# Two unsplit blocks ahead of the units in a feed-forward network, and GpSimd additions in its norm (Trainium2)

## The chip, the cores and the metric

The kernel runs on one core of one Trainium2 chip. The metric is the device time of one execution in microseconds (us); lower is better. Three runs of the kernel before gave 1261.36, 1261.36 and 1261.72 us, median 1261.36 us.

## The reference

Two layers of a decoder run on 16 learned meta tokens followed by 512 tokens (528 columns), width 1024. Each layer normalises `h`, projects it once for a forgetting-attention group (8 heads) and a retention group (4 heads), joins both groups through an output projection that is added to `h`, and adds a gated feed-forward network of width 2816. All arithmetic is float32.

```python
xn = rmsnorm(h, attn_norm_g)
proj = xn @ w_in                          # q, k, v of both groups, gates
mix = concat(fox_attention(...), silu(rg) * head_groupnorm(retention(...)))
h = h + mix @ w_out
hn = rmsnorm(h, ffn_norm_g)
ff = silu(hn @ w_gate) * (hn @ w_up)      # 1024 -> 2816
h = h + ff @ w_down                       # after layer 2: rmsnorm, meta tokens dropped
```

## The kernel before, in words

**Layout.** `h` lies transposed: eight tiles `h0` to `h7` of 128 features by 528 columns. Every float32 operand is split into a rounded part (type fp32r, names ending in `hi` or `h`) and the rest (`lo`, `l`), and each product is three TensorE matmuls: hi by hi, hi by lo, lo by hi. In layer 0 a pass over the 528 columns is two matmuls of 264 columns; in layer 1, where the meta tokens are no longer needed, it is one of 512.

**Weights.** A weight block of 128x1024 arrives by DMA in a tile `raw`. ScalarE casts it into `whi` (L199), and VectorE, or GpSimd where `dense_steps` was called with `pool`, subtracts to give `wlo` (L202; GpSimd in pieces of 128 columns). `convert` does this for the next block while a block is multiplied (L225); `ahead=(1, 4)` says at which of its steps.

**Feed-forward network.** The 2816 features are 22 blocks of 128. The first `PLAIN` blocks are plain: the gate product and the up product, eight steps of k each. Each later block is a `Unit`, in which gate and up share work in the manner of Strassen and Winograd: seven products of four chunks with three matmuls each over half of the columns (264 or 256), 84 matmuls in all. `head` uses `x` as it is; `middle` and part of `tail` need the four token forms `th`, `tl`, which `x_forms` (L883 and following) makes from `h` on ScalarE and VectorE; the weight sums of a unit (`make2` to `make4`, L961 and following) are VectorE's too. Blocks are grouped in `ROUNDS`; while one round is computed, the blocks of the round before are multiplied by `w_down` (`down`, L1065), a pair of output tiles for each unit. At the end of layer 1 the last round is `down` in two column parts of 272 and 240 (L930), with the final norm beside it.

**The norm of the feed-forward network.** `squares` takes the eight squares of `h` on ScalarE (L352, L357) and sums them by seven additions into `ss` on VectorE (L361). `sqh` and `sql`, the split of that sum, go through a matmul with ones (L304) that TensorE meets after the twelfth step of the network. `scale_split` makes `xh` (ScalarE, L339) and `xl` (VectorE, L341), the split input; step k of the first block needs `xh` and `xl` of tile k. `add_h` (L832, L829) has just added the output projection to `h`. `squares` is called with `att=False` in three places: for the feed-forward norm of layer 0 and of layer 1, and for the attention norm of layer 0 at the very start of the program, where it is also pinned in program order. The attention norm of layer 1 passes `att=True`.

**What sets the order.** TensorE runs its instructions in the order in which the steps are written; the other engines' orders come from the scheduler, by priority, and each engine executes its own queue strictly in order. Pools of tiles with a fixed number of buffers make a writer wait for the readers of the buffer's last content: three for `raw`, two for `whi` and `wlo`, four for the group of temporaries that holds `sq`. In PSUM, `psum()` (L267) hands out two buffers of a pair of banks, `psd`, and `psum_a()` (L270) four single banks, `psa`. A unit's two sums that `middle` and `tail` share accumulate in one `psd` pair, from its head to its `done`, where VectorE reads it (L1006, `sg`). The second `down` of a fill takes a `psd` pair as well; the first takes two `psa` banks in layer 0, by its last argument, and a `psd` pair in layer 1.

## Time and profile before

| | |
|---|---|
| median of three runs | 1261.36 us |
| the profiled execution | 1261.38 us, its span 1259.6 us |
| TensorE busy | 1248.7 us, 9225 matmuls |
| VectorE busy | 989.2 us |
| ScalarE busy | 706.6 us |
| GpSimd busy | 281.6 us |

In the profile PE is TensorE, PEld its weight loads, DVE VectorE, ACT ScalarE, POOL GpSimd and SP the engine that issues most DMAs. Times are us from the start of the span, which is 1.8 us shorter than the time of the execution. Matmuls overlap: a row's duration is longer than the distance to the next one, and the distance is what a matmul costs. A row of the timeline gives the start, the length, the engine and line, what is written and read, and how many instructions it merges; idle time in front stands in brackets with what ended it. Layer 0's feed-forward network starts at 281.6 us, layer 1's at 903.3 us.

### The profile page before, as it was taken

How to read it: one execution, taken by the hardware profiler on the slowest of the kernel's cores; microseconds unless marked ns; L12 is line 12 of the kernel's file. 1: busy time of each engine (PE TensorE's matmuls, PEld its weight loads, DVE VectorE, ACT ScalarE, POOL GpSimd, SP SyncE). 2: the span in 40 equal slices, each digit the busy share in tenths (PEclk: the TensorE clock that was granted, in tenths of full speed). 3: DMA queues.
4: the chain of work that ended last, by engine and by line, in shares of the span. 5: the costliest groups of instructions: out<-in, count | busy, mean ns of one | idle time of the engine just before them, and what ended most of it. 6: DMA issues, size and time to landing. Idle time of an engine off the chain costs nothing.

```text
span 1259.6 us, 23534 instructions
## 1 busy us (share of the span) xinstructions
PE 1248.7 (99%) x9225; PEld 1191.9 (95%) x9225; DVE 989.2 (79%) x1786; ACT 706.6 (56%) x1307; POOL 281.6 (22%) x552
## 2 busy tenths in 40 slices
PE   9999999999999999999999999999999999999997
PEld 8999999999999999999999988998789999999996
DVE  7887756789888888887786876567899888888867
ACT  7767655776454444444466665557764444444445
POOL 4545655420000000000125556554100000000000
PEclk9999999999999999999999999999999999999999
DMA  6222222123233323332322222221333333333322
GB/s 219 68 76 71 74 68 90 55 81 117 93 102 103 96 100 101 101 101 85 103 75 84 76 77 70 82 77 51 130 95 111 101 101 101 100 101 101 101 84 67
DMA packets 43342, 116.19 MB, mean 92 GB/s; under 512 B 5088, under 2 KB 12000, under 8 KB 43232
## 3 DMA queue, kind: packets, MB, share of 16 engines
q1 hardware_dynamic: 42800, 114.41, 28.4%
q8 instruction: 72, 1.18, 0.4%
q14 instruction: 38, 0.31, 0.1%
q10 hardware_dynamic: 432, 0.29, 0.1%
HBM read 112.58 MB, written 2.10 MB: 91 GB/s over the span
## 4 chain that ended last, share of the span: by engine, by line
PE 95%; DVE 3%; ACT 2%; DMA 0%; issue 0%; ACTq 0%; DVEq 0%
PE psd L225 31%; PE psa L930 18%; PE psd L1065 14%; PE psd L930 13%; PE psa L225 5%; PE psa L1065 4%; PE psa L441 2%; PE psa L608 2%; PE psa L538 1%; PE psa L742 1%; PE psa L778 1%; PE psa L402 1%; PE psa L304 0%; DMA raw<-w_in 0%; PE psa L617 0%
## 5 line engine op out<-in xcount | busy, mean ns | idle before, releaser
L202 POOL TENSOR_TENSOR wlo<-raw,whi 128x128 fp32r<-128x128 f32 x504 | 262.4, 555 | 243.0 <-ACT whi L199 220.9
L225 PE MATMUL psd<-xh,whi 128*128 128x264 f32 (+1 forms) x792 | 195.2, 314 | 0.1
L225 PE MATMUL psd<-xh,wlo 128*128 128x264 f32 (+1 forms) x792 | 186.6, 303 | 0.0
L225 PE MATMUL psd<-xl,whi 128*128 128x264 f32 (+1 forms) x792 | 186.2, 302 | 0.2 <-DVE xl L341 0.2
L225 PEld LDWEIGHTS psd<-xh,wlo 128*128 128x128 f32 x792 | 126.8, 188 | 6.3 <-DVE wlo L202 0.4
L225 PEld LDWEIGHTS psd<-xh,whi 128*128 128x128 f32 x792 | 128.1, 189 | 4.9 <-ACT whi L199 0.6
L225 PEld LDWEIGHTS psd<-xl,whi 128*128 128x128 f32 x792 | 127.3, 188 | 4.8 <-DVE xl L341 0.9
L199 ACT CAST whi<-raw 128x512 fp32r<-128x512 f32 (+1 forms) x168 | 98.2, 613 | 42.9 <-PE psd L225 29.2
L918 ACT CAST whi<-raw 128x1024 fp32r<-128x1024 f32 (+2 forms) x62 | 54.9, 885 | 51.3 <-PE psd L930 39.8
L918 ACT CAST fwhi<-raw 128x1024 fp32r<-128x1024 f32 (+2 forms) x62 | 55.6, 897 | 47.5 <-PE psd L930 40.0
L122 POOL MEMSET kc<- 64x528 f32 x4 | 2.1, 533 | 345.6 <-PE psa L930 345.4
L919 DVE TENSOR_TENSOR wlo<-raw,whi 128x1024 fp32r<-128x1024 f32 (+2 forms) x62 | 62.9, 1015 | 12.3 <-ACT whi L918 12.2
L919 DVE TENSOR_TENSOR fwlo<-raw,fwhi 128x1024 fp32r<-128x1024 f32 (+2 forms) x62 | 64.0, 1032 | 10.1 <-ACT fwhi L918 10.0
L930 PE MATMUL psa<-th,whi 128*128 128x264 f32 (+1 forms) x232 | 65.4, 282 | 0.0
L930 PE MATMUL psa<-th,wlo 128*128 128x264 f32 (+1 forms) x232 | 65.4, 282 | 0.0
L930 PE MATMUL psa<-tl,whi 128*128 128x264 f32 (+1 forms) x232 | 65.3, 282 | 0.0
L930 PE MATMUL psa<-th,fwhi 128*128 128x264 f32 (+1 forms) x224 | 63.4, 283 | 0.0
L930 PE MATMUL psa<-tl,fwhi 128*128 128x264 f32 (+1 forms) x224 | 63.3, 283 | 0.0
L930 PE MATMUL psa<-th,fwlo 128*128 128x264 f32 (+1 forms) x224 | 63.2, 282 | 0.0
L555 ACT ACTIVATE pr<-pr,nmax 128x144 f32<-128x144 f32 (+1 forms) x64 | 36.8, 576 | 45.5 <-DVE nmax L542 26.0
L918 ACT CAST fwhi<-S 128x1024 fp32r<-128x1024 f32 x20 | 21.0, 1049 | 68.6 <-PE psa L930 66.5
L996 ACT COPY e<-psa 128x264 f32<-128x264 f32 (+1 forms) x114 | 42.8, 375 | 28.3 <-PE psa L930 24.1
(366 smaller groups left out, 4041.1 us busy)
## 6 DMA issues: line engine op xcount, KB each, us to landing
raw<-w_in SPq DMA_DIRECT2D x54, 512.0 KB, 3.5
raw<-w_gate SPq DMA_DIRECT2D x44, 512.0 KB, 3.9
fraw<-w_up SPq DMA_DIRECT2D x38, 512.0 KB, 3.5
raw<-w_down SPq DMA_DIRECT2D x64, 256.0 KB, 2.9
raw<-w_out SPq DMA_DIRECT2D x16, 512.0 KB, 3.5
raw<-w_down SPq DMA_DIRECT2D x32, 192.0 KB, 2.5
raw<-w_up SPq DMA_DIRECT2D x6, 512.0 KB, 3.5
h<-x_t SPq DMA_DIRECT2D x8, 264.0 KB, 4.9
```

Source lines behind the costliest of these rows:

```text
L199: pin(nc.scalar.copy(hi, job["raw"][:, c0:c1]), pinned)
L202: pin(sub(lo[:, c:c + step], job["raw"][:, c0 + c:c0 + c + step], hi[:, c:c + step].bitcast(F32)), pinned)
L225: nc.tensor.matmul(ps[1][b][:, 0:c1 - c0], w[:, wk, :], x[:, c0:c1], start=(k == 0 and i == 0), stop=(k == n - 1 and i == 2))
L402: nc.tensor.matmul(ps[:, 0:c1 - c0], wf[k // HB][:, k % HB, :], st["x"][k][part][:, c0:c1], start=(i == 0), stop=(i == 2 * NK - 1))
L441: nc.tensor.transpose(ps[:, 128 * j:128 * j + 128], src[:, o:o + 128], idt)
L555: nc.scalar.activation(pr, pr, AF.Exp, bias=nmax[0:nq], scale=-1.0, accum_out=rsum)
L608: nc.tensor.matmul(po[:, c0:SEQ], v[:, j, :], pp[:, j, META + c0:T], start=(j == 0 and i == 0), stop=(j == 4))
L918: nc.scalar.copy(hi, src)
L919: nc.vector.tensor_sub(lo, src, hi.bitcast(F32))
L930: nc.tensor.matmul(bank()[:, 0:b.shape[-1]], a[:, o + k, :], b, start=(fresh and k == 0 and i == 0), stop=(k == n - 1 and i == 2), skip_gr ...
L996: nc.scalar.copy(self.t["e"][:, i], self.t["x"][:, 0:w])
L1065: nc.tensor.matmul(v[:, 0:c1 - c0], a[:, s * n + k, :], b[:, c0:c1], start=(k == 0 and i == 0), stop=(k == n - 1 and i == 2))
```

## The change

- `PLAIN` goes from 3 to 2, so block 2 becomes a unit in both layers, and the rounds become one of two blocks and five of four (before: 3, 4, 4, 4, 4, 3).
- The heads of the first two units are both issued before the first `middle`; the code that carried a unit's tail over to the next one goes, since there are always `down` fills.
- `x_forms` are inserted every seven steps, not nine.
- In `squares`, where `att` is false, the additions of squares 1 to 5 go to GpSimd; 6 and 7 stay on VectorE.
- `whi` and `wlo` get three buffers; blocks marked `far` convert the weights two blocks ahead; the third `w_out` block of the second round is subtracted on GpSimd. The second sums of the first unit are made at high priority.
- Of the `down` fills, the first for each of the first two units of layer 1 uses two banks and halves of 256 columns.

```diff
-ROUNDS = ((0, 3), (3, 7), (7, 11), (11, 15), (15, 19), (19, 22))
-PLAIN = 3
+ROUNDS = ((0, 2), (2, 6), (6, 10), (10, 14), (14, 18), (18, 22))
+PLAIN = 2
...
-        return pool.tile([128, NK, 128], F32R, name=tag, tag=tag, bufs=2)
+        return pool.tile([128, NK, 128], F32R, name=tag, tag=tag, bufs=2 if tag[0] == "f" else 3)
...
-                [(NK, *[wp.tile([128, NK, 128], F32R, name=i, tag=i) for i in ("whi", "wlo")])]
+                [(NK, *[wring(i) for i in ("whi", "wlo")])]
...
                         convert(j + 1, 4 * half + 4)
+                        if far:
+                            convert(j + 2, 4 * half + 4)
...
                 with ExitStack() if att else tc.high_priority():
-                    nc.vector.tensor_add(acc[:, c], acc[:, c], sq[:, c])
+                    (nc.vector if att or k > 5 else nc.gpsimd).tensor_add(acc[:, c], acc[:, c], sq[:, c])
...
-                                rnd == 0 or m2 < 2, rnd == 1 and m2 == 1) for m2 in range(NK // 2)], [])
+                                rnd == 0 or m2 < 3, rnd == 1 and m2 == 1, far=rnd == 1 and m2 > 1) for m2 in range(NK // 2)], [])
...
-                nc.vector.tensor_add(s[:, HB:NK], b[:, 0:HB], b[:, HB:NK])
-                nc.vector.tensor_sub(s[:, 0:HB], s[:, HB:NK], a[:, 0:HB])
-                splits(hi, lo, s)
+                with tc.high_priority() if self.f == PLAIN else ExitStack():
+                    nc.vector.tensor_add(s[:, HB:NK], b[:, 0:HB], b[:, HB:NK])
+                    nc.vector.tensor_sub(s[:, 0:HB], s[:, HB:NK], a[:, 0:HB])
+                    splits(hi, lo, s)
...
-                u = Unit(f)
-                steps += u.head()
-                for v in tails:
-                    v.last()
-                    steps += v.tail()
-                tails = []
+                for i in (f, f + 1) if f == PLAIN else (f,):
+                    if i not in units:
+                        units[i] = Unit(i)
+                        steps += units[i].head()
+                u = units[f]
                 u.rest()
                 steps += u.middle()
...
+                steps += down(j, 0, 2 * p, g0, g1, not real or f < PLAIN + 2)
...
-            steps.insert(NK + 4 + 9 * i, x_forms(i))
+            steps.insert(NK + 4 + 7 * i, x_forms(i))
```

The first place is VectorE at the start of the program, the sum of the squares for layer 0's attention norm (`ss` is the sum, `sq` a square, `mxl` the low part of the third weight block, `sql` the low part of the sum). Before:

```order
L361 TENSOR_TENSOR ss_217<-ss_217,sq_219 128x528
L361 TENSOR_TENSOR ss_217<-ss_217,sq_222 128x528
L361 TENSOR_TENSOR ss_217<-ss_217,sq_225 128x528
L361 TENSOR_TENSOR ss_217<-ss_217,sq_228 128x528
L396 TENSOR_TENSOR pick_83<-idt_81 40x8
L361 TENSOR_TENSOR ss_217<-ss_217,sq_231 128x528
L361 TENSOR_TENSOR ss_217<-ss_217,sq_234 128x528
L202 TENSOR_TENSOR mxl0_329<-raw_326,mxh0_328 128x512
L361 TENSOR_TENSOR ss_217<-ss_217,sq_237 128x528
L202 TENSOR_TENSOR mxl1_331<-raw_326,mxh1_330 128x512
L295 TENSOR_TENSOR sql_337<-ss_217,sqh_336 128x528
```

The same place on VectorE with the change:

```order
L398 TENSOR_TENSOR pick_83<-idt_81 40x8
L363 TENSOR_TENSOR ss_217<-ss_217,sq_234 128x528
L363 TENSOR_TENSOR ss_217<-ss_217,sq_237 128x528
L202 TENSOR_TENSOR mxl0_329<-raw_326,mxh0_328 128x512
L202 TENSOR_TENSOR mxl1_331<-raw_326,mxh1_330 128x512
L297 TENSOR_TENSOR sql_337<-ss_217,sqh_336 128x528
```

Five additions have left VectorE, and both `mxl` subtractions now stand between the last addition and `sql`.

On GpSimd these five additions are one chain, each reading the sum that the one before wrote; they stand behind its memsets and ahead of its first weight subtractions.

The second place is VectorE where layer 0's feed-forward network starts (`xl` is the low part of the network's input, `wlo` that of a weight block, `h6` and `h7` the last two tiles of the residual). Before:

```order
L832 TENSOR_TENSOR h6_79<-psd_4056,h6_79 128x528
L361 TENSOR_TENSOR ss_4183<-ss_4183,sq_4197 128x528
L202 TENSOR_TENSOR wlo_4072<-raw_4069,whi_4071 128x512
L341 SCALAR_TENSOR_TENSOR xl2_4129<-h2_75,vec_84,xh2_4128 128x528
L361 TENSOR_TENSOR ss_4183<-ss_4183,sq_4200 128x528
L832 TENSOR_TENSOR h7_80<-psd_4088,h7_80 128x528
L341 SCALAR_TENSOR_TENSOR xl3_4133<-h3_76,vec_84,xh3_4132 128x528
L341 SCALAR_TENSOR_TENSOR xl4_4137<-h4_77,vec_84,xh4_4136 128x528
L341 SCALAR_TENSOR_TENSOR xl5_4141<-h5_78,vec_84,xh5_4140 128x528
L361 TENSOR_TENSOR ss_4183<-ss_4183,sq_4203 128x528
L341 SCALAR_TENSOR_TENSOR xl6_4145<-h6_79,vec_84,xh6_4144 128x528
L341 SCALAR_TENSOR_TENSOR xl7_4149<-h7_80,vec_84,xh7_4148 128x528
```

The same place on VectorE with the change:

```order
L343 SCALAR_TENSOR_TENSOR xl3_4147<-h3_76,vec_84,xh3_4146 128x528
L343 SCALAR_TENSOR_TENSOR xl4_4151<-h4_77,vec_84,xh4_4150 128x528
L834 TENSOR_TENSOR h6_79<-psd_4070,h6_79 128x528
L343 SCALAR_TENSOR_TENSOR xl5_4155<-h5_78,vec_84,xh5_4154 128x528
L343 SCALAR_TENSOR_TENSOR xl6_4159<-h6_79,vec_84,xh6_4158 128x528
L363 TENSOR_TENSOR ss_4197<-ss_4197,sq_4214 128x528
L834 TENSOR_TENSOR h7_80<-psd_4102,h7_80 128x528
L202 TENSOR_TENSOR wlo_4182<-raw_4179,whi_4181 128x512 x2
L894 TENSOR_TENSOR S_4303<-S_4303 128x264
L343 SCALAR_TENSOR_TENSOR xl7_4163<-h7_80,vec_84,xh7_4162 128x528
```

The addition of square 6, which waits for GpSimd's fifth, now stands ahead of `h7`, and two `wlo` subtractions of the second gate block and a row of a token form stand between `h7` and `xl7`.

The third place is VectorE where the first unit of layer 0 ends (`S`, `raw` and `fraw` hold weight sums of the units, `wlo` and `fwlo` their low parts, `e` and `sg` belong to the unit's `done`, `h0` is added from the first `down`). Before:

```order
L964 TENSOR_TENSOR S_4916<-fraw_4874 128x512
L919 TENSOR_TENSOR fwlo_4700<-raw_4695,fwhi_4699 128x1024
L999 TENSOR_TENSOR e_4629<-psd_4631,e_4629 128x264
L977 TENSOR_TENSOR raw_4695<-raw_4695,S_4739 128x512
L965 TENSOR_TENSOR S_4916<-S_4916,raw_4872 128x512
L1070 TENSOR_TENSOR h0_73<-psa_4703,h0_73 128x264
L1070 TENSOR_TENSOR h0_73<-psa_4704,h0_73 128x264
L971 TENSOR_TENSOR fraw_4874<-raw_4872,fraw_4874 128x512
L919 TENSOR_TENSOR wlo_4738<-S_4739,whi_4737 128x1024
L1006 TENSOR_TENSOR sg_4756<-psd_4631,e_4629 128x528
```

The same place on VectorE with the change:

```order
L921 TENSOR_TENSOR wlo_4614<-S_4615,whi_4613 128x1024
L921 TENSOR_TENSOR wlo_4695<-raw_4691,whi_4694 128x512
L1002 TENSOR_TENSOR e_4514<-psd_4516,e_4514 128x264
L980 TENSOR_TENSOR raw_4486<-raw_4486,S_4615 128x512
L1073 TENSOR_TENSOR h0_73<-psa_4620,h0_73 128x264
L1073 TENSOR_TENSOR h0_73<-psa_4621,h0_73 128x264
L967 TENSOR_TENSOR S_4780<-fraw_4744 128x512
L968 TENSOR_TENSOR S_4780<-S_4780,raw_4742 128x512
L974 TENSOR_TENSOR fraw_4744<-raw_4742,fraw_4744 128x512
L921 TENSOR_TENSOR fwlo_4649<-fraw_4488,fwhi_4648 128x1024
L1009 TENSOR_TENSOR sg_4665<-psd_4516,e_4514 128x528
```

In both, weight rows of the next units stand between `e` and the read of the unit's pair by `sg`; with the change they are those of the third unit, and by then the pairs of the first two units are both in use.

More of the change, by code (lines that the diff above doesn't have):

```diff
@@ L203, in convert, with dense_steps @@
             job["split"] = c1
-    def dense_steps(src, parts, pool=False, banks=False, ahead=(1, 4), own=None, wait=None):
+    def dense_steps(src, parts, pool=False, banks=False, ahead=(1, 4), own=None, wait=None, far=False):
         j = len(jobs)
@@ L1076, in ffn @@
         steps = []
-        tails = []
         fills = []
+        units = {}
         for r, (f0, f1) in enumerate(ROUNDS):
@@ L1081, in ffn @@
                 if f < PLAIN:
[L1082 to L1083 removed]
+                    steps += dense_steps(w_gate[l, f], [(0, xs, NK, QC, g_done(f) if f else held.append)], banks=f == 1, far=True)
+                    steps += dense_steps(w_up[l, f], [(0, xs, NK, QC, u_done(f))], far=f == 0)
                     continue
[L1085 to L1090 removed]
+                for i in (f, f + 1) if f == PLAIN else (f,):
[3 more added lines that the diff above has]
+                u = units[f]
                 u.rest()
                 steps += u.middle()
[L1093 to L1102 removed]
+                p, g0, g1 = fills.pop(0)
                 j = down_job(p, g0, g1)
[L1104 to L1105 removed]
+                steps += down(j, 0, 2 * p, g0, g1, not real or f < PLAIN + 2)
+                u.last()
+                steps += u.tail()
+                steps += down(j, 1, 2 * p + 1, g0, g1, False)
             fills = [(p, f0, f1) for p in range(NK // 2)]
```

15 lines of the change are left out of this document (removed).

## The prediction

> **What bounds the kernel now.** I read the page's busy times, then the chain that ended last, then TensorE's own waits.
>
> ```profile
> span 1259.6 us, 23534 instructions
> PE 1248.7 (99%) x9225; PEld 1191.9 (95%) x9225; DVE 989.2 (79%) x1786; ACT 706.6 (56%) x1307; POOL 281.6 (22%) x552
> PE 95%; DVE 3%; ACT 2%; DMA 0%; issue 0%; ACTq 0%; DVEq 0%
> PE psa L1300 <- DVE wide L62: 1.6, 1, 1.6
> ...
> PE psd L225 <- DVE xl L341: 0.2, 1, 0.2
> ```
>
> TensorE is the bound nearly everywhere: 95% of the chain is its own, and the longest of its listed waits is 1.6 us, at the very start, the shortest 0.2 us for an `xl`. So the time is the sum of its matmuls, and two things can move it: fewer columns, or new waits. At 99% busy there is hardly a wait left to remove; any that the change makes is added whole.
>
> **TensorE's work.** The cost of a matmul is its distance to the next. Two pieces of the chain give it for 264 and 256 columns, two rows of the timeline for 512.
>
> ```profile
> 317.31 1.45 PE psa L930 x12
> 1000.00 1.41 PE psa L930 x12
> 895.25 0.39 PE L225 MATMUL psd<-mxh,whi 128*128 128x512 f32 x1
> 895.48 0.39 PE L225 MATMUL psd<-mxl,whi 128*128 128x512 f32 x1
> ```
>
> That is 0.121, 0.118 and 0.230 us. In layer 0 a plain block is 16 steps of six matmuls, 96, and a unit is 84: -12 x 0.121 = -1.45 us. In layer 1 it is 48 of 512 columns against 84 of 256: -48 x 0.230 + 84 x 0.118 = -1.13. The last round, split in 272 and 240 columns, has a fourth block: 24 matmuls of each width for 24 of 512; and two fills of layer 1 go from 12 matmuls of 512 columns to 24 of 256. Between the same two points (0.44 ns a column) that is 24 x (0.125 + 0.111 - 0.230) + 12 x (0.236 - 0.230) = +0.22. Sum **-2.4 us**, 0.19% of the time: all that the change can take off the bound.
>
> **The squares at the start.** `squares` without `att` is layer 0's attention norm too, so five additions go to GpSimd there as well. Its rows on VectorE and TensorE:
>
> ```profile
> 14.40 3.14 DVE L361 TENSOR_TENSOR ss<-ss,sq 128x528 f32<-128x528 f32 x4 [0.34 <-ACT sq L357]
> 19.09 0.68 DVE L202 TENSOR_TENSOR mxl<-raw,mxh 128x512 fp32r<-128x512 f32 x1
> 19.69 0.70 DVE L361 TENSOR_TENSOR ss<-ss,sq 128x528 f32<-128x528 f32 x1
> 21.09 0.71 DVE L295 TENSOR_TENSOR sql<-ss,sqh 128x528 fp32r<-128x528 f32 x1
> 21.89 0.47 PE L304 MATMUL psa<-sql,ones 128*128 128x264 f32 x2
> ```
>
> `sql` ends at 21.80 and TensorE reads it at 21.89: no slack, and TensorE can pass nothing in front. What does an addition of 528 columns take on GpSimd? No row has one. Nearest are its subtractions of 128 columns and its memsets; below them two stretches of VectorE, without and with GpSimd at work beside it.
>
> ```profile
> 45.94 0.46 POOL L202 TENSOR_TENSOR wlo<-raw,whi 128x128 fp32r<-128x128 f32 x1 [1.67 <-ACT whi L199]
> L386 POOL MEMSET mxh<- 128x512 f32 x2 | 1.0, 522 | 6.0 <-PE psd L1065 6.0
> L101 POOL MEMSET pth<- 128x80 f32 x2 | 0.3, 170 | 0.0
> 28.22 0.69 DVE L468 SCALAR_TENSOR_TENSOR tq<-tq,R 128x528 f32<-128x528 f32 x1
> 28.84 0.68 DVE L421 TENSOR_SCALAR z<-z,bfg 8x528 f32<-8x528 f32 x1
> 80.22 4.43 POOL L202 TENSOR_TENSOR wlo<-raw,whi 128x128 fp32r<-128x128 f32 x6
> 81.28 0.85 DVE L807 TENSOR_TENSOR d<-d,sg 128x528 f32<-128x528 f32 x1
> ...
> 83.93 0.77 DVE L318 SCALAR_TENSOR_TENSOR nwt<-psa,nwt 128x264 f32<-128x264 f32 x2
> ```
>
> A subtraction of 128 columns takes 0.46 us. If the columns beyond 128 cost what a memset's do ((522 - 170)/432 = 0.81 ns), an addition is 0.46 + 400 x 0.81 ns = 0.78 us; if all of it grows with the columns, 0.46 x 528/128 = 1.90. The last rows lie between. A VectorE row with two SBUF operands takes 28.84 - 28.22 = 0.62 us from start to start; beside GpSimd three of them take 83.93 - 81.28 = 2.65 us, 0.79 more, and GpSimd's six take 4.43 us instead of 6 x 0.46 = 2.76. The two hold each other up. Some three of GpSimd's six lie beside those three rows, so each costs VectorE 0.26 us, 2.06 ns a column. I take that as what a column occupies: an addition is 0.46 + 400 x 2.06 ns = **1.28 us**, and 528 x 2.06 ns = 1.09 of it shut VectorE out. The Trainium skill ("GPSIMD Engine Reference", section 3.1) gives 4497 ns for a two-operand operation of 2048 columns, by which an addition is an estimated 1.16 us; by it this term is 0.6 less, and so is the sum.
>
> Each addition needs the one before. VectorE's chain shows the distance of two dependent ones: (3.14 - 0.70)/3 = 0.81, so 0.1 us beyond an addition. Five at 1.38 from 14.40 end at 21.3, two on VectorE at 22.9. Then come both `mxl` rows, 0.60 each (19.69 - 19.09), of which only one stood behind the last addition before; `sql` ends at 24.7 and TensorE reads it at 24.8 for 21.89. All that follows hangs on this norm: **+2.9 us**. At 0.78 us an addition it is +0.4, at 1.90 +6.
>
> **Where the feed-forward networks start.** In a network's first block, step 7 needs `xl7`. Layer 0, then layer 1:
>
> ```profile
> 273.12 0.70 DVE L832 TENSOR_TENSOR h<-psd,h 128x528 f32<-128x528 f32 x1
> 285.33 1.44 DVE L341 SCALAR_TENSOR_TENSOR xl<-h,vec,xh 128x528 fp32r<-128x528 f32 x2
> 286.98 0.40 PE L225 MATMUL psd<-xl,whi 128*128 128x264 f32 x2
> 895.49 0.68 DVE L832 TENSOR_TENSOR h<-psd,h 128x512 f32<-128x512 f32 x1
> 907.35 1.41 DVE L341 SCALAR_TENSOR_TENSOR xl<-h,vec,xh 128x512 fp32r<-128x512 f32 x2
> 908.95 0.40 PE L225 MATMUL psd<-xl,whi 128*128 128x512 f32 x1
> ```
>
> `xl7` ends at 286.77 for a read at 286.98, and at 908.76 for one at 908.95. VectorE's rows here, grouped by shape over the stretch from 268 to 300 us (busy time, mean duration in ns):
>
> ```profile
> L202 DVE TENSOR_TENSOR wlo<-raw,whi 128x512 fp32r<-128x512 f32 x12 | 7.9, 684 | 0.0
> L341 DVE SCALAR_TENSOR_TENSOR xl<-h,vec,xh 128x528 fp32r<-128x528 f32 x8 | 5.8, 761 | 0.0
> L151 DVE TENSOR_TENSOR tl<-S,th 128x1056 fp32r<-128x1056 f32 x2 | 2.5, 1258 | 0.0
> L894 DVE SCALAR_TENSOR_TENSOR S<-h,vec,S 128x264 f32<-128x264 f32 x4 | 1.8, 482 | 0.0
> L892 DVE TENSOR_TENSOR S<-S 128x264 f32<-128x264 f32 x3 | 1.3, 424 | 0.0
> ```
>
> From start to start a row costs 0.08 us less than its duration (two `xl` of 0.76 end after 1.44). From `h4` at 273.1 to `xl7` the new queue has eight `xl` (0.68), four `h` and one `ss` (0.62), four `wlo` (0.60) and a half form row (0.34): 11.3 us, done at 284.5 if nothing interferes. But GpSimd's five additions fall here, since square 5 needs `h5`. They shut VectorE out for 5 x 1.09 = 5.5 us at the most. Off that go some 0.9 us beside `h` rows, whose second operand is in PSUM, and 0 to 1.6 us beside moments when VectorE waits for TensorE's next residual anyway: 3.0 to 4.5 us lost, and I take the middle, **3.7**. `xl7` then ends at 288.2 and TensorE reads it 1.3 us late. The addition of square 6, which waits for GpSimd's fifth, stands ahead of `h7` in VectorE's queue, and so behind it stand `xh7` and `xl7` for GpSimd.
>
> That wait doesn't decide, because VectorE is still as late some 37 us further on, where TensorE meets it again. Both heads are now issued first, and each unit holds a pair of `psd` banks from its head to its `done`, where VectorE reads it (`sg`). The pool has two pairs. So the second `down` beside the first unit finds none free until VectorE has read the first unit's pair. In the kernel before, only one unit lived then, and that `down` (L1065) began before the read:
>
> ```profile
> 329.25 1.23 DVE L919 TENSOR_TENSOR wlo<-S,whi 128x1024 fp32r<-128x1024 f32 x1 [1.05 <-ACT whi L918]
> 329.52 0.41 PE L1065 MATMUL psd<-ah,fwhi 128*128 128x264 f32 x2
> 330.39 0.70 DVE L1006 TENSOR_TENSOR sg<-psd,e 128x528 f32<-128x528 f32 x1
> ```
>
> When does VectorE come to that read? Its new queue has, from behind `xl7` to the end of `sg`, 12 rows of 528 columns (0.62), 12 three-operand rows of 264 (0.40) and 10 others of 264 (0.34), 4 of 1056 (1.18), 6 of 1024 (1.15), 16 of 512 (0.60): 36.9 us, so it ends at 288.2 + 36.9 = 325.1. When does TensorE ask? Without any wait: step 7 ends at 287.5, 24 steps of 6 x 0.121 follow, the ones matmuls (0.49), two heads and the `middle` of 28 chunks (3 x 0.121 each), a `down` of 12 matmuls (1.45) and the tail (8 chunks, 2.9): 287.5 + 17.4 + 0.5 + 10.2 + 1.45 + 2.9 = 319.9. So TensorE gets on at 325.1, and the 1.3 us for `xl7` are part of this lag: **+5.2 us** for layer 0 (nothing lost to GpSimd: 284.5 + 36.9 - 319.9 = +1.5; 4.5 lost: +6.0). Even a VectorE with nothing else to do costs 0.8, since `sg` (0.70) can't begin before the tail ends.
>
> Layer 1 in the same way: from 895.5, eight `xl`, five more and four `wlo` rows of 512 columns make 13 - 2.3 = 10.6 us, done at 906.1, and with 3.6 lost at 909.7. Then 10 rows of 1024, 27 of 512 (six of them with three operands) and 19 of 256 columns, 35.0 us: 944.7. TensorE, from the read at 908.95, takes 24 steps of 3 x 0.230, 0.46, 28 chunks and 8 more of 3 x 0.118 and a `down` of 1.42, on top of the 0.46 left of step 7: 940.6. **+4.1 us** (+0.8 to +5.0).
>
> The rest costs nothing. The last token form is done some 25 us after `xl7`, at 313.3, about when the fourth chunk of the `middle` reads it; slack is gone there, not exceeded. The 8 pieces of the third `w_out` block go to GpSimd ahead of the additions, 8 x 0.46 = 3.7 us that end before `h1` is there. The conversions two blocks ahead are counted as `wlo` rows. In SP's queue weight transfers of the second and third block move by a few places, and TensorE's listed waits name VectorE and ScalarE alone, no DMA.
>
> **The end.** Four blocks in the last round give VectorE a third more time per tile beside the final norm.
>
> ```profile
> 1249.82 1.89 PE L1187 MATMUL psa<-S,ones 128*128 128x240 f32 x8 [0.21 <-ACT S L1158]
> 1253.90:1259.00 5.10, 0.00 (x0) 0.00 (x0) 2.04 (x4) 0.00 (x0) 0.00 (x0) 0.50 0.65 216
> ```
>
> The 0.21 us and about as much in front may go: **-0.4** (0 to -0.7).
>
> **Sum:** -2.4 + 2.9 + 5.2 + 4.1 - 0.4 = +9.4 us on the profiled execution's 1261.38 (0.02 above the median): **1270.8 us**. Its own range, from the ends of what GpSimd shuts out, is 1268.5 to 1273.
>
> **The rivals.**
>
> *GpSimd stays out of VectorE's way.* Nothing is shut out, an addition takes 0.78 to 1.28 us: -2.4 + (0.4 to 2.9) + 1.5 + 0.8 - 0.4 gives 1261.3 to 1263.8, no measurable change. For it: the stretch at 81 us is a single one, and its rows are not of the new kind. Against it: both engines are slow there at once. Chance 0.22.
>
> *VectorE is early enough.* The side that is not slower: additions at 0.78 us, and VectorE's rows from `h4` to `sg` 2 us shorter than the 48 that I count, so that `sg` begins as the tail ends. It decides there: 319.9 in layer 0. Then -2.4 + 0.4 + 2 x 0.8 - 0.4, and layer 1's present wait at `xl7` (0.2 in the list of waits) gone as well: -1.0, 1260.4 us. For it: the distances from start to start are from a stretch where VectorE never paused. Against it: each idle moment of VectorE for ScalarE (1.05 us in the row at 329.25) goes the other way. Chance 0.12, of which a third for small terms that I have too dear by the 1.6 us still missing to a gain that shows.
>
> *The clock falls.* The last row quoted shows the granted clock at 0.50 from 1253.9, 2.2 us after the last matmul (1249.82 + 1.89). A single wait of 4 or 5 us may set that off in mid-kernel; if what runs slowly afterwards is as long as those 2.2 to 5 us, half of it is lost, 1.1 to 2.5 us a fall: with three waits 1273 to 1277. The Trainium skill ("TensorE: Matmul & The Clock Gate", "What's actually happening") has the clock judged over free-running windows of about 3.4 us, so that by it a wait of 4 to 5 us would lose an estimated 1.7 us if it covers one. Chance 0.10.
>
> My forecast has 0.40, and 0.16 lies between it and the first rival, with 1 to 3 us shut out in each network: 1264 to 1268.5.
>
> **How the numbers follow.** A measurement of this kernel can tell about 0.2%, 2.5 us, from no change: 1258.8 to 1263.9. Faster has a third of the second rival, 0.04; the same has the rest of it and the first, 0.30; slower the others, 0.66. The range leaves out the faster cases, the clock's and the top of the forecast's own: 1260.0 to 1273.
>
> **What would show it.** Right: seven `ss` rows split five on POOL and two on DVE; POOL rows of about 1.3 us at 14 us and longer ones at 275 us; a PE wait of nearly 3 us for `sql` at 22 us, and 3 to 5 us in front of the second L1065 group of both networks, released by VectorE's `sg`; distances between matmuls as before. Wrong: POOL additions under 0.9 us, `xl` rows of 0.76 us beside them, that `down` running before `sg`, or a first `middle` that waits for `tl`.

## The result, and the profile after

The changed kernel takes **1282.18 us** (median of 4 runs, 1278.06 to 1282.79) against 1261.46 before: a ratio of 1.0156, 95% interval 1.0138 to 1.0174. That is 20.7 us slower. The forecast was 1270.8, with a range up to 1273: the sign was right, the size less than half. The lowest of the four runs, at a mean granted clock of 0.998 where the others have 0.993, lies above the range too.

The page's first lines and the shares of the chain that ended last, then TensorE's own waits (total, count, longest, in us):

```profile
span 1280.3 us, 23639 instructions
PE 1255.1 (98%) x9285; PEld 1200.0 (94%) x9285; DVE 991.9 (77%) x1784; ACT 710.1 (55%) x1313; POOL 316.6 (25%) x583
PE 86%; DVE 9%; ACT 2%; issue 1%; DMA 1%; POOL 0%; DVEq 0%; ACTq 0%; SPq 0%; POOLq 0%
```

```profile
PE psd L225 <- DVE h L834: 4.0, 2, 2.7
PE psd L1068 <- DVE sg L1009: 3.8, 2, 2.0
PE psa L932 <- ACT ah L150: 2.2, 1, 2.2
PE psa L1295 <- DVE wide L62: 1.6, 1, 1.6
PE psd L1068 <- ACT ah L150: 1.4, 1, 1.4
PE psa L306 <- ACT sqh L296: 1.4, 1, 1.4
PE psa L306 <- DVE sql L297: 0.6, 1, 0.6
PE psd L225 <- DVE sg L867: 0.6, 1, 0.6
```

VectorE's share of the chain went from 3% to 9%, and where the list had one line over 0.5 us it now has seven more. Each norm's ones matmuls are a mark that both traces have. The time of the first one (us), and how far the changed kernel is behind:

| mark | before | after | behind | added since |
|---|---|---|---|---|
| attention norm of layer 0, first mark | 21.65 | 23.70 | 2.05 | 2.05 |
| second mark of layer 0 | 78.88 | 82.79 | 3.9 | 1.9 |
| last mark before layer 0's network | 257.00 | 260.89 | 3.9 | 0.0 |
| layer 0's network, after its twelfth step | 290.58 | 298.83 | 8.25 | 4.4 |
| first mark of layer 1 | 644.23 | 656.23 | 12.0 | 3.75 |
| last mark before layer 1's network | 879.85 | 891.57 | 11.7 | -0.3 |
| layer 1's network, after its twelfth step | 912.41 | 925.51 | 13.1 | 1.4 |
| final norm | 1244.15 | 1263.53 | 19.4 | 6.3 |
| last matmul's end | 1251.71 | 1272.30 | 20.6 | 1.2 |

The projections and attention (rows with 0.0 and -0.3) are untouched. All of the loss is at the program start, with the stretch of slow clock behind it, and in the two networks.

**Program start.** GpSimd's five additions, VectorE's rest of the sum, TensorE's reads, and the clock in the stretch behind:

```profile
14.48 6.95 POOL L363 TENSOR_TENSOR ss<-ss,sq 128x528 f32<-128x528 f32 x5 [8.76 <-ACT sq L359]
```

```profile
21.46 1.52 DVE L363 TENSOR_TENSOR ss<-ss,sq 128x528 f32<-128x528 f32 x2 [5.63 <-POOL ss L363]
24.11 0.70 DVE L297 TENSOR_TENSOR sql<-ss,sqh 128x528 fp32r<-128x528 f32 x1
```

```profile
23.70 0.51 PE L306 MATMUL psa<-sqh,ones 128*128 128x264 f32 x2 [1.42 <-ACT sqh L296]
24.86 0.51 PE L306 MATMUL psa<-sql,ones 128*128 128x264 f32 x2 [0.65 <-DVE sql L297]
```

Five additions take 6.95 us, 1.39 each with the step to the next one, where 1.38 was worked out, and TensorE reads `sql` at 24.86 for the 24.8 of the forecast. Behind the two waits the granted clock falls, which the forecast had only as a rival.

**Layer 0's network.** GpSimd's additions, what VectorE does beside them, and the first matmul of the network's first block:

```profile
278.28 4.86 POOL L363 TENSOR_TENSOR ss<-ss,sq 128x528 f32<-128x528 f32 x3 [8.57 <-ACT sq L359]
284.02 3.18 POOL L363 TENSOR_TENSOR ss<-ss,sq 128x528 f32<-128x528 f32 x2 [0.89 <-ACT sq L359]
```

```profile
277.68 4.27 DVE L343 SCALAR_TENSOR_TENSOR xl<-h,vec,xh 128x528 fp32r<-128x528 f32 x3
281.87 0.70 DVE L834 TENSOR_TENSOR h<-psd,h 128x528 f32<-128x528 f32 x1
282.49 1.80 DVE L202 TENSOR_TENSOR wlo<-raw,whi 128x512 fp32r<-128x512 f32 x2
284.21 3.55 DVE L343 SCALAR_TENSOR_TENSOR xl<-h,vec,xh 128x528 fp32r<-128x528 f32 x2
287.69 0.69 DVE L834 TENSOR_TENSOR h<-psd,h 128x528 f32<-128x528 f32 x1
```

```profile
288.53 0.59 PE L225 MATMUL psd<-xh,whi 128*128 128x264 f32 x2 [2.67 <-DVE h L834]
```

Undisturbed, three `xl` end after 2.12 us (2 x 0.68 + 0.76), two `wlo` after 1.28 and two `xl` after 1.44. So VectorE loses 2.15 + 0.52 + 2.11 = 4.8 us to five additions, 0.96 each. An addition done by VectorE itself costs it 0.62. TensorE doesn't wait for `xl7`, though, but for a PSUM pair: the first block takes a `psd` pair, both are held by tiles of the output projection, and `h6`'s read at 287.69 stands in VectorE's queue behind the stretched `xl`. Later VectorE keeps to the count of the forecast: from behind `xl7` to the end of `sg` it takes 37.1 us (293.41 to 330.54) for 36.9.

**First unit, and last unit.** The read of the first unit's pair and TensorE behind it in layer 0, then TensorE at the last unit's activation in layer 1 and ScalarE's row that makes it (`ah`):

```profile
328.71 1.22 DVE L921 TENSOR_TENSOR fwlo<-fraw,fwhi 128x1024 fp32r<-128x1024 f32 x1
329.84 0.70 DVE L1009 TENSOR_TENSOR sg<-psd,e 128x528 f32<-128x528 f32 x1
```

```profile
330.60 0.51 PE L1068 MATMUL psd<-ah,whi 128*128 128x264 f32 x2 [2.03 <-DVE sg L1009]
1246.32 0.39 PE L932 MATMUL psa<-ah,whi 128*128 128x272 f32 x1 [2.16 <-ACT ah L150]
1245.65 0.62 ACT L150 CAST ah<-tq 128x512 fp32r<-128x512 f32 x1 [0.25 <-DVE tq L1017]
```

In the kernel before, that activation (`ah`, `al`) was ready over 2 us ahead of its read, behind a fill that was over:

```profile
1229.12 0.62 ACT L150 CAST ah<-tq 128x512 fp32r<-128x512 f32 x1
1230.13 0.68 DVE L151 TENSOR_TENSOR al<-tq,ah 128x512 fp32r<-128x512 f32 x1
1232.87 0.29 PE L930 MATMUL psa<-ah,whi 128*128 128x272 f32 x1
```

The `sg` wait is the forecast's, in its place. The last was not in the forecast at all: four fills go with four units, so nothing is over behind the last unit, and the final `down`s read its activation before ScalarE and VectorE have made it.

**The clock.** Four stretches of the view by windows (the third figure from the end is the granted clock):

```profile
26.00:28.00 2.00, 2.00 (x9) 2.00 (x10) 1.03 (x2) 1.97 (x5) 2.00 (x4) 0.50 0.52 209
290.00:292.00 2.00, 2.00 (x11) 2.00 (x11) 2.00 (x4) 2.00 (x5) 0.00 (x0) 0.50 0.03 8
958.00:960.00 2.00, 2.00 (x9) 1.71 (x8) 1.42 (x4) 1.68 (x2) 0.00 (x0) 0.50 0.93 301
1248.00:1250.00 2.00, 2.00 (x11) 2.00 (x11) 0.09 (x2) 0.84 (x2) 0.00 (x0) 0.50 0.03 8
```

Each follows 1.8 to 2.7 us of waiting; the 2.03 us for `sg` in layer 0 are followed by none. At half clock TensorE does 9 to 11 matmuls in 2 us; at 0.121 us each it would be 16.

### The profile page after: what moved, and what is told of

Read it like the earlier page. It is cut to its first block, busy times and chain, and to the rows that moved or that the text cites. A ratio compares the mean times of both kernels' runs of the same rounds, so it can differ in the third digit from the quotient of the medians.

```text
span 1280.3 us, 23639 instructions
## 1 busy us (share of the span) xinstructions
PE 1255.1 (98%) x9285; PEld 1200.0 (94%) x9285; DVE 991.9 (77%) x1784; ACT 710.1 (55%) x1313; POOL 316.6 (25%) x583
## 4 chain that ended last, share of the span: by engine, by line
PE 86%; DVE 9%; ACT 2%; issue 1%; DMA 1%; POOL 0%; DVEq 0%; ACTq 0%; SPq 0%; POOLq 0%
PE psd L225 24%; PE psa L932 19%; PE psd L1068 13%; PE psd L932 13%; PE psa L225 4%; PE psa L1068 4%; PE psa L443 2%; PE psa L610 2%; PE psa L540 2%; PE psa L744 1%; DVE xl L343 1%; DVE wlo L202 1%; PE psa L780 1%; DVE fwlo L921 1%; DVE wlo L921 1%
## 5 line engine op out<-in xcount | busy, mean ns | idle before, releaser
L202 POOL TENSOR_TENSOR wlo<-raw,whi 128x128 fp32r<-128x128 f32 x520 | 274.8, 562 | 560.7 <-ACT whi L199 553.6
L225 PE MATMUL psd<-xh,whi 128*128 128x264 f32 (+1 forms) x744 | 183.1, 314 | 4.7 <-DVE h L834 4.0
L225 PE MATMUL psd<-xl,whi 128*128 128x264 f32 (+1 forms) x744 | 174.2, 302 | 0.3 <-DVE xl L343 0.2
L225 PE MATMUL psd<-xh,wlo 128*128 128x264 f32 (+1 forms) x744 | 174.2, 303 | 0.0
L920 ACT CAST whi<-raw 128x1024 fp32r<-128x1024 f32 (+1 forms) x64 | 57.0, 890 | 102.5 <-PE psa L932 65.2
L921 DVE TENSOR_TENSOR wlo<-raw,whi 128x1024 fp32r<-128x1024 f32 (+1 forms) x64 | 65.2, 1019 | 30.8 <-ACT whi L920 30.7
L920 ACT CAST fwhi<-raw 128x1024 fp32r<-128x1024 f32 (+1 forms) x64 | 57.0, 890 | 51.5 <-PE psd L932 39.5
L921 DVE TENSOR_TENSOR fwlo<-raw,fwhi 128x1024 fp32r<-128x1024 f32 (+1 forms) x64 | 65.1, 1018 | 6.0 <-ACT fwhi L920 6.0
L1068 PE MATMUL psd<-ah,whi 128*128 128x264 f32 (+1 forms) x180 | 50.7, 331 | 5.3 <-DVE sg L1009 3.8
L1075 DVE TENSOR_TENSOR h<-psd,h 128x512 f32<-128x512 f32 (+1 forms) x66 | 45.7, 693 | 12.7 <-PE psd L1068 12.7
```

The lines of the kernel that those rows point to most:

```text
L202: pin(sub(lo[:, c:c + step], job["raw"][:, c0 + c:c0 + c + step], hi[:, c:c + step].bitcast(F32)), pinned)
L225: nc.tensor.matmul(ps[1][b][:, 0:c1 - c0], w[:, wk, :], x[:, c0:c1], start=(k == 0 and i == 0), stop=(k == n - 1 and i == 2))
L920: nc.scalar.copy(hi, src)
L921: nc.vector.tensor_sub(lo, src, hi.bitcast(F32))
L1068: nc.tensor.matmul(v[:, 0:c1 - c0], a[:, s * n + k, :], b[:, c0:c1], start=(k == 0 and i == 0), stop=(k == n - 1 and i == 2))
L1075: nc.vector.tensor_add(sv(h[m], real), pv(ps[0], real), sv(h[m], real))
```

## The experiments

The theory after the result: the loss is a sum of separate causes (additions at the start, additions beside VectorE in the networks, the pair that two heads hold, the missing last fill), each with a share of slow clock. The rival: VectorE simply has too much to do with two plain blocks, and its debt moves from place to place.

**All additions on VectorE** (changed kernel):

```diff
-                    (nc.vector if att or k > 5 else nc.gpsimd).tensor_add(acc[:, c], acc[:, c], sq[:, c])
+                    nc.vector.tensor_add(acc[:, c], acc[:, c], sq[:, c])
```

> The changed kernel with all seven additions of the squares on VectorE, in all three places; nothing else differs. Theory (the additions on GpSimd do the harm at the program start and at both network starts): the 3.9 us at the program start go, the 2.7 us wait for h6 in layer 0 and the 1.4 us in layer 1 go with the slow clock behind the first, and VectorE, with 5 x 0.62 = 3.1 us of additions in place of some 4.9 us shut out, comes 1.8 us earlier to the read of the first unit's pair, so the two waits of 2.0 us there shrink below 0.5 us; the waits behind the last units (1.6 and 2.5 us) stay. 1282 - 3.9 - 4 - 2 - 3 = 1269 us, 1267 to 1273. Rival (VectorE is late by its new order, two heads and conversions two blocks ahead, wherever the additions are done): only the program start's 3.9 us go, 1277 to 1279 us.

Measured 1279.23 us (1278.43 to 1280.34; ratio to before 1.0127 to 1.0157): just above the rival's 1277 to 1279, though not in the rival's way. The start's loss and the waits for `h6` went, as the theory had it, but the waits for `sg` shrank only to 1.5 us, and a new one came in both networks:

```profile
PE psa L932 <- DVE fwlo L921: 7.7, 2, 4.5
PE psd L1068 <- DVE sg L1009: 3.0, 2, 1.5
```

This was the open question from here on: a debt, or one row in a bad place.

**The start alone on VectorE** (changed kernel): `if att or pinned or k > 5`.

> The changed kernel with the additions on VectorE at the program start alone; in both network norms five stay on GpSimd. Theory: 3.9 us less, 1278 us (1277 to 1279), TensorE reads sql near 21.9 us as before the change, and all later waits keep their lengths, the one for h6 (2.7 us) among them. Rival (the network starts suffer from what the start has shifted, or the additions in the networks are harmless): 1270 us or less, like the run with all additions on VectorE.

1278.90 us (1276.03 to 1281.04), inside the theory's range: 3.3 us less, and the later waits keep their lengths (2.7 us for `h6`, 2.2 for `sg`). The runs scatter by 5 us, with mean clocks from 0.992 to 0.998, so the trace is the better measure: by the last mark before layer 0's network it is 3.0 us less. It is not the whole 3.9, in part because a wait of 0.6 us appears near 37 us, in front of the first attention product; the three-buffer run below comes back to it.

**The last fill behind the tail** (changed kernel):

```diff
-                j = down_job(p, g0, g1)
-                steps += down(j, 0, 2 * p, g0, g1, not real or f < PLAIN + 2)
+                late = f == NF - 1
+                j = None if late else down_job(p, g0, g1)
+                if not late:
+                    steps += down(j, 0, 2 * p, g0, g1, not real or f < PLAIN + 2)
                 u.last()
                 steps += u.tail()
+                if late:
+                    j = down_job(p, g0, g1)
+                    steps += down(j, 0, 2 * p, g0, g1, not real)
```

> The changed kernel in which the last unit's fill puts both of its downs behind the tail, in both layers, so that 2.9 us more of TensorE's work lie between the last unit's end and the first matmul that reads its activation. Theory (with four fills for four units no fill is left to cover the activation of the last unit): the waits for ah and al at 628 us (1.6 us) and at 1244 us (2.5 us) go, and the slow clock at 1248 us with them: 2.0 + 2.9 + 1.7 less, 1275.5 us (1274.5 to 1277). Rival (the wait moves in front of the tail, whose weights are then late, or the chain of VectorE and ScalarE behind sg is longer than 2.9 us): under 3 us less, 1279 to 1282 us.

1275.37 us (1274.66 to 1276.06): 6.8 us less, the theory's 1275.5. No wait for `ah` or `al` is left; 0.5 us in front of the tail came in each layer. Of the 6.8, some 1.7 seem to be luck: this trace has no slow clock behind layer 1's wait for `sg`, though that wait is as long as before (1.8 us). The moved fill itself accounts for about 5 us: the waits that went, less those that came, and the slow clock at 1248 us.

**The additions in the kernel before:** the changed line of `squares` alone.

> The kernel before with one line of the change alone: five of the seven additions on GpSimd wherever the attention flag is off, three places. Theory: +3.9 us at the program start, as in the changed kernel, and at each network start VectorE is shut out for 4.5 to 5 us where it had 0.2 us to spare, less the 3.1 us of additions that it no longer does: +1.5 to +2 us each, with up to 1.7 us of slow clock each: 1261.4 + 3.9 + 3 to 7 = 1268 to 1272 us. Rival (the harm in the networks needs the new order, above all the two heads ahead): +3.9 us alone, 1265 us.

1270.94 us (ratio 1.0061 to 1.0091): +9.6, the theory's range. By the same marks its profiled execution, the slowest of the four, loses 3.8 at the start, 4.4 in layer 0's network and 1.4 in layer 1's up to the twelfth step, and 1.0 more behind that. TensorE's two longest waits there stand in the changed kernel too (4.0 and 1.4), so they need neither two heads nor two plain blocks:

```profile
PE psd L225 <- DVE h L832: 4.0, 2, 2.7
PE psa L304 <- ACT sqh L294: 1.9, 1, 1.9
```

**Two plain blocks in the kernel before:** `PLAIN = 2`, nothing else.

> The kernel before with PLAIN = 2 alone: block 2 is a unit in the first round of three blocks; one head at a time, nothing converted two blocks ahead, the additions on VectorE, one fill over at the end. Theory (with two plain blocks TensorE reaches the first unit 11.6 us sooner than VectorE, which has no idle moment from 270 to 320 us before the change, can prepare it): TensorE waits 3 to 5 us in each network for a first unit's weight part or a token form, 1261.4 - 2.6 + 6 to 10 and up to 2 x 1.7 of slow clock = 1265 to 1272 us. Rival (the waits come from what else changed in the order, the two heads and the conversions): waits under 1 us in all, 1259 to 1260 us.

1281.31 us, +19.9: dearer than either side expected, as dear as the whole change. TensorE waits mostly for token forms, which the old order brings too late, and 8.5 us are slow clock behind these waits:

```profile
PE psa L930 <- ACT th L150: 8.0, 2, 4.4
PE psa L930 <- DVE tl L151: 1.6, 2, 0.8
```

So the other parts of the change do pay for something: they remove these waits. They bring others of the same sum.

**One head ahead** (changed kernel): `for i in (f,):` in place of the pair at `PLAIN`.

> The changed kernel without the second head ahead of the first middle, all else as changed (five additions on GpSimd). Rival of mine from the prediction (the pair of banks that the second unit holds is what costs): the two waits of 2.0 us for sg go and nothing takes their place, 1276 to 1278 us. Theory (VectorE is late by what it has to do, and the pair is only where TensorE meets it): the first middle comes 2.9 us sooner and waits for a token form or a second weight part for 2 to 5 us in each network, 1280 to 1286 us.

1281.24 us (1279.81 to 1283.53), the theory's number, by another way than it said: both waits for `sg` L1009 are gone, and in their place stand 1.8 us for a plain block's pair in layer 0 (`sg` L867), 0.8 each for a weight part, and a slow stretch of the clock (0.61 from 312 to 316 us). The number is in part chance: at the program start, which the edit doesn't touch, this execution waited 2.1 us for `sqh` instead of 1.4 and had slow clock for 6.8 us instead of 3.4.

**Single banks for the second down beside the first unit** (changed kernel):

```diff
-                steps += down(j, 1, 2 * p + 1, g0, g1, False)
+                steps += down(j, 1, 2 * p + 1, g0, g1, f == PLAIN)
```

> The changed kernel in which the second down beside the first unit takes two single banks instead of a pair. If the held pair costs by itself: the waits of 2.0 us for sg at 328 and 955 us go, and at least once the slow clock behind them, 1276 to 1278 us. If VectorE's lateness is what counts: the wait moves to the next thing that VectorE owes (the first down's additions into h, the second unit's second weight part), within 1 us of the same length, 1280 to 1283 us.

1276.50 us (1275.87 to 1277.03), 5.7 less: both waits for `sg` (2.0 and 1.8 us) went, the slow clock at 958 us too, and nothing took their place. The held pair costs by itself.

**Three repairs together** (additions on VectorE, last fill late, single banks):

> The changed kernel with three repairs: all additions on VectorE, the last unit's fill behind its tail, and two single banks for the second down beside the first unit. Theory: 1279.2 (additions on VectorE) - 6.8 (last fill, as measured on the changed kernel) = 1272.5 us, less 0 to 3.4 for the two sg waits of 1.5 us that were left: 1269 to 1273 us; the waits of 3.4 and 4.7 us for the second head's low weights stay, so it does not come back to 1261 us. Rival (the three causes are all there is): 1259 to 1262 us.

1272.92 us, inside the theory's range. What is left is mainly the waits for the second head's low weights, 3.2 and 4.5 us, with slow clock behind both.

**Additions on VectorE, last fill late, one head:**

> The changed kernel with all additions on VectorE, the last unit's fill behind its tail, and one head ahead instead of two, so that the second down finds a free pair; two plain blocks, new rounds and three weight buffers stay. Theory (VectorE has some 3.5 us of work too much ahead of the first unit's middle, in either order of the heads): it waits about 1.7 us for the middle's low weights and 0.7 us further on in layer 0, somewhat more in layer 1, with a slow clock after one of them: 1261.4 - 2.4 + 0.8 (three buffers) + 1.3 (last unit) + 5 to 8 = 1266 to 1269 us, better than with two heads (1272.9) but not below the kernel before. Rival (one head suffices once the additions are VectorE's): 1260 to 1262 us.

1266.75 us (1266.35 to 1266.87), inside the theory's range; behind the program's first one no wait of over 1 us is left, and the clock stays at 1.00 until the last matmul. About 2 us in layer 0 and 3 in layer 1 are lost in small waits, mostly for weight parts and a form.

**Three buffers in the kernel before:** `bufs=3` for `whi` and `wlo`.

> The kernel before with three buffers for whi and wlo in place of two, nothing else. Theory (the 0.8 us that the changed kernel loses near 37 us, in front of the first product of the attention, come from ScalarE's order, in which the copies of pd now stand ahead of a weight cast): +0.6 to +0.9 us, 1262.0 to 1262.3 us. Rival (they come from the additions or the moved third weight block): 1261.4 us, no change.

1265.62 us (ratio 1.0020 to 1.0039). The wait near 37 us came as expected, with 0.6 us: with a third buffer ScalarE makes its two `pd` copies ahead of a weight cast, where they stood behind it before, and by the profile TensorE's first attention product waits for that cast. Why it waits for a weight is not shown. But the price is larger than the theory's, because the same freedom makes a wait of 2.1 us for layer 1's `sqh`, which the changed kernel doesn't have:

```profile
PE psa L304 <- ACT sqh L150: 2.1, 1, 2.1
```

ScalarE's rows show where it comes from. The cast of `mxh`, a weight of the forget gates, waits for GpSimd's memset of that tile, which now stands behind eight weight subtractions, and `sqh` stands behind the cast. In the changed kernel GpSimd's order is the same, but `sqh` stands ahead of that cast.

```profile
646.09 0.22 ACT L150 CAST mxh<-wfr 128x32 fp32r<-128x32 f32 x1 [3.71 <-POOL mxh L386]
646.22 0.63 ACT L150 CAST sqh<-ss 128x528 fp32r<-128x528 f32 x1
```

**Three plain blocks in the changed kernel:** `PLAIN = 3`, the fourth fill done behind the first round of units.

> The changed kernel with PLAIN = 3 again and the fill that is then over behind the first round of units; rounds, two heads, additions on GpSimd and all else as changed. Theory (two plain blocks leave VectorE too little time): the 2.5 us matmul gain is lost, the waits for sg at both first units (2.0 each), for the up block's pair in layer 1 (0.8) and one slow clock go, while the program start, the waits for h6 and those behind the last units stay: 1282 + 2.6 - 4.8 - 1.7 = 1278 us, 1277 to 1280. Rival (the two heads cause the waits by the pair they hold, whatever VectorE's lead): the waits for sg stay, 1283 to 1285 us.

1282.84 us, next to the rival's 1283 to 1285: the theory fell. With a whole plain block more for VectorE to catch up, TensorE still waits for `sg`, 1.5 us in each layer where it was 2.0 and 1.8:

```profile
PE psd L1068 <- DVE sg L1009: 3.0, 2, 1.5
```

VectorE is not behind there. In layer 0 its row ahead of `sg` has itself waited for a cast:

```profile
340.16 1.23 DVE L921 TENSOR_TENSOR fwlo<-fraw,fwhi 128x1024 fp32r<-128x1024 f32 x1 [1.15 <-ACT fwhi L920]
341.30 0.70 DVE L1009 TENSOR_TENSOR sg<-psd,e 128x528 f32<-128x528 f32 x1
```

So most of that wait is made by the held pair and by the place of `sg` behind weight rows, not by a debt.

**The three separate costs out** (start on VectorE, last fill late, single banks; the networks' additions stay on GpSimd):

> The changed kernel without its three costs that single runs showed: the program start's additions on VectorE (-3.3), the last unit's fill behind its tail (-6.8), two single banks for the second down beside the first unit (-5.7). The additions in both network norms stay on GpSimd, two heads and two plain blocks stay. Theory (the three are separate, each in its own place): they add up, 1282.2 - 15.8 = 1266.4 us (1265 to 1268); what is left over the kernel before is the wait for h6 and its like at both network starts with a slow clock, 4.4 + 1.5 + 0.8 us, and 0.7 us near 37 us, less 2.4 of columns. Rival (VectorE's lateness is one debt that moves from place to place, as when the additions went to VectorE): the gains overlap, 1270 to 1274 us.

1267.66 us (1267.39 to 1268.42), inside the theory's range: 14.5 of the 15.8 add up. It is 5.3 less than the three repairs with the additions on VectorE, although GpSimd's additions take more from VectorE than they save. The rows show why. The second head's low weights are made early here, and with the additions on VectorE 16.7 us later (layer 1 of this run, then of the run with three repairs):

```profile
921.28 1.21 DVE L921 TENSOR_TENSOR fwlo<-raw,fwhi 128x1024 fp32r<-128x1024 f32 x1
```

```profile
937.96 1.22 DVE L921 TENSOR_TENSOR fwlo<-raw,fwhi 128x1024 fp32r<-128x1024 f32 x1
```

**That row moved alone** (the three repairs, additions on VectorE):

```diff
             def make1(self, hi, lo):
-                splits(hi, lo, self.t["a"])
+                with tc.high_priority() if self.f == PLAIN + 1 else ExitStack():
+                    splits(hi, lo, self.t["a"])
```

> The kernel of the run with three repairs (additions on VectorE, last fill late, single banks for the second down; 1272.9 us) with one edit more: the first weight part of the second unit is made at high priority, which puts its low half 12 rows behind xl7 in VectorE's queue instead of 38. If the wait was a matter of that row's place: the waits of 3.4 and 4.7 us in the second head and the slow clock behind each go, and no more than 1 to 2 us in each network come back at the middle: 1262 to 1265 us. If VectorE is in debt by that much: the waits move to the middle's low weights at the same length, 1269 us or more.

1263.68 us (1263.29 to 1263.88): 9.2 us by one row's place in a queue; 5.1 us of slow clock behind the two long waits went with them. (The edit raises the cast in front of that row too, but in the run with three repairs the cast in layer 1 was done at 921 us already, 17 us ahead of the row.) The longest waits that are left:

```profile
PE psa L1301 <- DVE wide L62: 1.6, 1, 1.6
PE psa L932 <- ACT e L1000: 0.9, 2, 0.5
PE psd L225 <- DVE sg L867: 0.9, 1, 0.9
PE psa L932 <- DVE fwlo L921: 0.8, 1, 0.8
```

It is the best version found and still 1.0015 of the kernel before (1.0006 to 1.0024).

**With two buffers again, and nothing converted two blocks ahead** (the kernel of the run before):

> The same with two buffers for whi and wlo and nothing converted two blocks ahead. Theory: the 0.7 us near 37 us come back, and in the networks the low weights of the second and third block come later on VectorE, which costs under 1 us: 0.5 us less than the run before it in this call to 0.5 more; 1261 to 1265 us. Rival (three buffers and the conversions two ahead are what keeps the second blocks' weights in time): a wait of 1 us or more for a plain block's low weights in each network.

1265.20 us, 1.5 more, where the theory had at most 0.5; the rival's waits for a plain block's low weights didn't come either. The wait near 37 us goes, and the 0.9 us for a plain block's pair in layer 0, but 1.0 us for such a pair and 1.3 us for the last unit's activation come in layer 1. The third buffers and the conversions two ahead, taken together, are worth more than they cost in this order.

## Why the prediction was wrong, by its own steps

- **Columns, -2.4:** right. The count of matmuls went up by 60 (9225 to 9285), as -12, +36, +24 and +12 of the forecast's sums give, and the network of layer 0 has the 12 fewer.
- **Program start, +2.9:** the wait came as worked out (24.86 for 24.8); the slow clock behind it made it 3.9.
- **Where the networks start, +5.2 and +4.1:** right in mechanism, wrong on one reader, and short by the clock. VectorE lost 4.8 us to the additions where 3.7 was taken (3.0 to 4.5 as bounds). TensorE met that first at `h6`'s pair, which the forecast overlooked; with the slow clock layer 0 lost 4.4 there and 2.2 at `sg`, 6.6 in all. Layer 1 lost 1.4, then 0.8 at a plain block's pair, 2.0 at `sg` and 1.7 of clock: 5.9. Without the clock that is 4.9 and 4.2, close to the forecast, but partly by luck, since a larger loss was met in other places.
- **"Even a VectorE with nothing else to do costs 0.8":** the pair was the right cause, shown by giving the second `down` other banks (-5.7). But the forecast made VectorE's backlog responsible for most of the length, and with three plain blocks 1.5 of the 2.0 us stayed without a backlog.
- **"The end", -0.4:** the step that failed. It counted what a fourth block gives the final norm (the wait of 0.2 us there is gone from the list) and didn't ask what had lain between the last unit and the reads of its activation: a fill that was over with three units and four fills. It cost 2.0 us in layer 0 and 2.9 plus 1.7 of clock in layer 1, 6.6 together. In the run with the fill put behind the tail these waits are gone. Of the steps this is the largest part of the 11.4 us that were missing.
- **The clock as a rival with 0.10:** it fell four times, 1.7 us each, 6.8 us of the 20.7. Its price was put beside the forecast; with a chance, it belonged into the price of every wait of about 2 us and more. Even so the forecast would have been too low, by about the 4.9 us of waiting at the last units.
- **The two rivals on the other side:** both asked for GpSimd to keep out of VectorE's way, and it doesn't: 0.96 us per addition, where 0.62 was saved. The second also took the 0.2 us wait for an `xl` to be at layer 1's `xl7`; in the trace before, it stands at 7.5 us, at the program start.

These terms add up to the 20.6 us of the last mark, but not stage by stage: by the marks layer 0's network lost 1.0 us more than they give and layer 1's 0.7 less, and no wait was found for that.

What is left open: why the scheduler's order of ScalarE and GpSimd shifts so with a third buffer, and why it put the second head's low weights so late once the additions were on VectorE. No version was tried that mends the small waits of the best one.

## What to carry to other kernels

When a change re-groups work into equal rounds, look for what the odd one out was covering: the piece that was over at the end may have been the only work between the last producer and its reader. A buffer taken earlier (a second head, a second pair) must be checked against its pool's size and against the place of its reader in another engine's queue. And work given to GpSimd isn't off VectorE's account when both read two operands from SBUF: price it by what VectorE loses beside it.

## What the runs showed of the hardware

- GpSimd's addition of two SBUF operands and VectorE's rows with two SBUF operands hold each other up. Five additions of 528 columns cost VectorE 4.8 us, 0.96 each. An `xl`, 0.76 us long by itself, took some 1.8 us beside an addition (two in 3.55 us), and an addition some 1.6 us beside VectorE's rows (three in 4.86) for 1.39 alone; the `h` row at 281.87 us, with one operand in PSUM, kept its 0.70. The Trainium skill ("SBUF — State Buffer", "SBUF: two separate sides") calls the shared ports an exclusive lock for a whole instruction, not a split of bandwidth; the rows agree.
- The wait of 2.7 us for `h6` was followed by half clock in all eight profiled kernels that had it, its like of 1.3 us in layer 1 in none. In between it differs from execution to execution: the 2.2 us for the last unit's activation were followed by it in three of six profiled kernels. The kernel with three buffers waits 2.1 us at one place, and its ten runs fall into four of 1264.0 to 1264.9 us and six of 1265.6 to 1266.2, at mean clocks of 0.998 and 0.997. Once even 3.2 us went without.
- A fall lasts about 3.4 us: granted 0.59 from 288 to 292 us and 0.98 from 292 to 296 in the changed kernel, (0.41 + 0.02) x 4 / 0.5 = 3.4. The Trainium skill ("TensorE: Matmul & The Clock Gate", "What's actually happening") gives that length, and a window that runs freely; but it puts the fall behind an idle window of that length, where here less was enough. The clock records of the traces show the grid: the four falls of the changed kernel begin at 25.92, 288.75, 957.76 and 1247.89 us, which is 77.0, 196.0 and 85.0 times 3.413 us apart.
- What decides, as far as these traces go, is how much of one window of that grid TensorE is idle. By the matmul records of the eleven traces with a fall inside the work, full clock ended behind all 20 windows with 2.0 us of idle time or more, behind 3 of 6 with 1.8 to 1.9 us, and behind 1 of 35 with 0.8 to 1.8. So a wait can go without a fall where an edge of the grid divides it. The 2.03 us for `sg` in the changed kernel are divided into 1.1 and 0.9; the 3.2 us that went without a fall (309.47 to 312.65 us, with all additions on VectorE) into 1.9 and 1.3. The scatter of the changed kernel's own runs, 1278.06 at a mean clock of 0.998 and 1282 at 0.993, fits this.
